# Retention heads two at a time on the full 128 partitions, with weights loaded ahead and filler matmuls in the chunk loop

## The chip, the cores and the metric

One Trainium2 chip, eight cores, each running the same program on its own prompt and its own 16 samples; the cores do not talk to each other. The metric is device time of the slowest core in microseconds (us). PE is the matmul engine, DVE the vector engine, ACT the scalar engine, POOL and SP the engines that here mostly issue transfers. The chip has two dies of four cores. In some executions the cores of a die run at a lower granted PE clock ("slow state") and the time is some per cent longer (in before's profiled run 6862.7 us at 0.777 on one die, 6735.6 us at 0.800 on the other).

## The reference, cut to what matters

Two layers of a decoder. Each layer is: half-step SwiGLU, token mixer (three head groups: gated delta net, a linear recurrent unit, retention), half-step SwiGLU. Only retention is touched. It has four heads of width 64:

```python
rq = rope(ret_q); rk = rope(ret_k) * 64 ** -0.5; rv = ret_v       # 4 heads x 64
o = exp(G) * (q @ S0) + ((q @ k.T) * decay_mask) @ v              # per chunk, G = cumulated log gamma
S = exp(G_C) * S0 + (k * exp(G_C - G)).T @ v                      # 64 x 64 state per head
o = (o - mean(o)) * rsqrt(var(o) + eps) * silu(ret_g)             # per head
out = concat(o_dn, o_lru, o_ret) @ w_out
```

A core has 2080 columns: 2064 prompt tokens (17 chunks, 16 + 16 x 128) and 16 one-token samples with states of their own.

## The kernel before: the parts that matter

Heads are processed one after another. Each uses 64 of the 128 partitions, so the projections fill 64 of the array's 128 columns, and most chunk matmuls 64 of its 128 rows. A fence (everything waits for the last instruction of every engine and every transfer) ends each head.

```python
for h in range(4):
    ...
    for (which, dst, name) in ((0, rq, "rq"), (1, rk, "rk")):       # q and k, with a swapped copy for the rotation
        sl = cnt["w"] % 2                                           # two weight buffers
        P.dma("pool", wring[:, sl, :, 0:64],   wiv[:, :, c0:c0 + 64], w=[("wr", sl)])
        P.dma("pool", wring[:, sl, :, 64:96],  wiv[:, :, c0 + 32:c0 + 64], r=[("wr", sl)], w=[("wr", sl)])
        P.dma("pool", wring[:, sl, :, 96:128], wiv[:, :, c0:c0 + 32], r=[("wr", sl)], w=[("wr", sl)])
        for ti, (a, n) in enumerate(TT):                            # 5 tiles of 416 columns
            for c in range(8): mm(pb[0:64, 0:n],  wring[:, sl, c, 0:64],   xn[:, c, a:a + n], ...)
            for c in range(8): mm(pb2[0:64, 0:n], wring[:, sl, c, 64:128], xn[:, c, a:a + n], ...)
            ...                                                     # three DVE operations: rotate
    def ret_chunk(ci, g):                                           # generator; three chunks in flight
        tr(bank[0:C, 0:64], rk[0:64, ...]); tr(bank[0:C, 64:128], rv[0:64, ...])
        mm(bank[0:C, 128:128 + C], rk[0:64, ...], rq[0:64, ...])    # scores
        yield
        ...                                                         # DVE: scaled k, v, masked scores
        while rturn["i"] != ci: yield                               # chunks take the state in turn
        mm(bank[0:64, 0:C], Sr, qp, start=True, stop=False)
        mm(bank[0:64, 0:C], vtm, MT, start=False, stop=True)
        mm(bank[0:64, 256:320], ktm, vtm)
        yield
        stt(Sr, Sr, gam ** C, bank[0:64, 256:320], ...)             # DVE: new state
        ...                                                         # norm: two means on PE, DVE, ACT
    run_pool(ret_chunk, 17, 3)
    ...                                                             # sample step, then the gate projection
    P.fence()
apply_wout([768, 832, 896, 960], 64)                                # four products over 64 rows
```

Of the kernel before, what the change touches and what calls it, by code (L numbers as in the profile page):

```python
# [10 lines left out]
AF = mybir.ActivationFunctionType  # L11
# [263 lines left out]
def build(stage=99):  # L275
# [18 lines left out]
    c_retdec = din("c_retdec", [4, 128, 128]); c_reteg = din("c_reteg", [64, 4, 128])  # L294
    c_retkd = din("c_retkd", [128, 8]); c_cos = din("c_cos", [64, NT]); c_sin = din("c_sin", [64, NT])
# [12 lines left out]
    with ExitStack() as st:  # L308
# [17 lines left out]
        def mm(out, lhsT, rhs, r, w, start=True, stop=True):  # L326
            P.op("pe", lambda e: e.matmul(out, lhsT, rhs, start=start, stop=stop), r, w)  # L327

# [158 lines left out]
        def mixer(l, xn):  # L487
# [8 lines left out]
            wiv = win[l].rearrange("(c p) n -> p c n", p=128)  # L496
            cnt = {"w": 0, "pre": 0, "tmp": 0, "st": 0}

            def load_w(col0, ncols):
                sl = cnt["w"] % 2  # L500
                cnt["w"] += 1
                P.dma("pool", wring[:, sl, :, 0:ncols], wiv[:, :, col0:col0 + ncols], w=[("wr", sl)])
                return sl

            def proj_tile(sl, ncols, ti):
                a, n = TT[ti]
                pb, kb = PB()
                for c in range(8):
                    mm(pb[0:ncols, 0:n], wring[:, sl, c, 0:ncols], xn[:, c, a:a + n], [("wr", sl), ("xn", ti)], kb,
                       start=(c == 0), stop=(c == 7))  # L510
                return pb, kb
# [444 lines left out]
            apply_wout([512, 640], 128)  # L956
            A.phase("lru")
# [9 lines left out]
            reteg = A.alloc([4, 128])  # L967
            P.dma("sp", reteg[0:64], c_reteg, w=["reteg"])
            for h in range(4):
                mh = A.mark()  # L970
                gam = 1.0 - 2.0 ** (-5.0 - h)
                mrr = AR.mark()
                rq = AR.alloc([NT]); rk = AR.alloc([NT]); rv = A.alloc([NT])
                decT = A.alloc([128])
                P.dma("sp", decT, c_retdec[h], w=["decT"])
                Sr = A.alloc([64])
                memset(Sr[0:64], 0.0, ["Sr"])
                tq_ = A.alloc([2, 512])
                for (which, dst, name) in ((0, rq, "rq"), (1, rk, "rk")):
                    c0 = 2568 + which * 256 + h * 64  # L980
                    sl = cnt["w"] % 2
                    cnt["w"] += 1
                    P.dma("pool", wring[:, sl, :, 0:64], wiv[:, :, c0:c0 + 64], w=[("wr", sl)])
                    P.dma("pool", wring[:, sl, :, 64:96], wiv[:, :, c0 + 32:c0 + 64], r=[("wr", sl)], w=[("wr", sl)])
                    P.dma("pool", wring[:, sl, :, 96:128], wiv[:, :, c0:c0 + 32], r=[("wr", sl)], w=[("wr", sl)])
                    for ti, (a, n) in enumerate(TT):
                        pb, kb = PB()
                        for c in range(8):
                            mm(pb[0:64, 0:n], wring[:, sl, c, 0:64], xn[:, c, a:a + n], [("wr", sl), ("xn", ti)], kb,
                               start=(c == 0), stop=(c == 7))  # L990
                        pb2, kb2 = PB()
                        for c in range(8):
                            mm(pb2[0:64, 0:n], wring[:, sl, c, 64:128], xn[:, c, a:a + n], [("wr", sl), ("xn", ti)], kb2,
                               start=(c == 0), stop=(c == 7))
                        s2 = ti % 2
                        rs = rcnt["i"] % 2
                        rcnt["i"] += 1
                        P.dma("sp", cosr[0:64, rs, 0:n], c_cos[:, a:a + n], w=[("cosr", rs)])
                        P.dma("sp", sinr[0:64, rs, 0:n], c_sin[:, a:a + n], w=[("sinr", rs)])
                        tt(tq_[0:64, s2, 0:n], pb[0:64, 0:n], cosr[0:64, rs, 0:n], ALU.mult, kb + [("cosr", rs)], [("tq", s2)])  # L1000
                        tt(dst[0:64, a:a + n], pb2[0:64, 0:n], sinr[0:64, rs, 0:n], ALU.mult, kb2 + [("sinr", rs)], ck(name, a, a + n))
                        tt(dst[0:64, a:a + n], dst[0:64, a:a + n], tq_[0:64, s2, 0:n], ALU.add, ck(name, a, a + n) + [("tq", s2)],
                           ck(name, a, a + n))
                sl = load_w(3080 + h * 64, 64)
                for ti, (a, n) in enumerate(TT):
                    pb, kb = proj_tile(sl, 64, ti)
                    cp(rv[0:64, a:a + n], pb[0:64, 0:n], kb, ck("rv", a, a + n), eng="act")

                RNG = 3
                rsets = [{k: A.alloc([128]) for k in ("qp", "ktm", "vtm", "MT", "o", "cen")} for _ in range(RNG)]  # L1010
                for T_ in rsets:
                    T_["sq"] = T_["o"]
                    T_["rn"] = T_["o"]
                RAL = {"sq": "o", "rn": "o"}

                def ret_post(o_src, ko, t0, C, T_, K, bank, kbk):
                    cp(T_["o"][0:64, 0:C], o_src, ko, K("o"))
                    yield
                    mm(bank[0:64, 0:C], o64, T_["o"][0:64, 0:C], K("o") + ["o64"], kbk)
                    yield  # L1020
                    tt(T_["cen"][0:64, 0:C], T_["o"][0:64, 0:C], bank[0:64, 0:C], ALU.subtract, K("o") + kbk, K("cen"))
                    tt(T_["sq"][0:64, 0:C], T_["cen"][0:64, 0:C], T_["cen"][0:64, 0:C], ALU.mult, K("cen"), K("sq"))
                    yield
                    mm(bank[0:64, 0:C], o64, T_["sq"][0:64, 0:C], K("sq") + ["o64"], kbk)
                    yield
                    ts(T_["rn"][0:64, 0:C], bank[0:64, 0:C], EPS, -0.5, ALU.add, ALU.pow, kbk, K("rn"))
                    yield
                    tt(oT[0:64, h, t0:t0 + C], T_["cen"][0:64, 0:C], T_["rn"][0:64, 0:C], ALU.mult, K("cen") + K("rn"),
                       ck(("oT", h), t0, t0 + C))
# [3 lines left out]
                def ret_chunk(ci, g):  # L1033
# [6 lines left out]
                    tt(T_["qp"][0:64, 0:C], rq[0:64, t0:t0 + C], reteg[0:64, h, 0:C], ALU.mult, kq_ + ["reteg"], K("qp"), eng="pool")  # L1040
                    tr(bank[0:C, 0:64], rk[0:64, t0:t0 + C], ident[0:64, 0:64], kk_ + ["ident"], kbk)
                    tr(bank[0:C, 64:128], rv[0:64, t0:t0 + C], ident[0:64, 0:64], kv_ + ["ident"], kbk)
                    mm(bank[0:C, 128:128 + C], rk[0:64, t0:t0 + C], rq[0:64, t0:t0 + C], kk_ + kq_, kbk)
                    yield
                    kcol = retkd[0:C, 2 * h + (0 if C == 128 else 1):2 * h + (0 if C == 128 else 1) + 1]
                    ts(T_["ktm"][0:C, 0:64], bank[0:C, 0:64], kcol, None, ALU.mult, None, kbk + ["retkd"], K("ktm"))
                    cp(T_["vtm"][0:C, 0:64], bank[0:C, 64:128], kbk, K("vtm"))
                    tt(T_["MT"][0:C, 0:C], bank[0:C, 128:128 + C], decT[0:C, 0:C], ALU.mult, kbk + ["decT"], K("MT"))
# [3 lines left out]
                    mm(bank[0:64, 0:C], Sr[0:64, 0:64], T_["qp"][0:64, 0:C], ["Sr"] + K("qp"), kbk, start=True, stop=False)  # L1052
                    mm(bank[0:64, 0:C], T_["vtm"][0:C, 0:64], T_["MT"][0:C, 0:C], K("vtm") + K("MT"), kbk, start=False, stop=True)
                    mm(bank[0:64, 256:320], T_["ktm"][0:C, 0:64], T_["vtm"][0:C, 0:64], K("ktm") + K("vtm"), kbk)
                    yield
                    stt(Sr[0:64, 0:64], Sr[0:64, 0:64], gam ** C, bank[0:64, 256:320], ALU.mult, ALU.add, ["Sr"] + kbk, ["Sr"])
                    rturn["i"] = ci + 1
                    yield from ret_post(bank[0:64, 0:C], kbk, t0, C, T_, K, bank, kbk)

                run_pool(ret_chunk, 17, RNG)  # L1060
                P.dma("sp", o_ret_p[l, h], Sr[0:64, 0:64], r=["Sr"], is_out=True)

# [4 lines left out]
                S0r = cosr.rearrange("p a (b c) -> p (a b) c", c=64)  # L1067
                Snr = sinr.rearrange("p a (b c) -> p (a b) c", c=64)
                KS0 = [("cosr", 0), ("cosr", 1)]
                KSN = [("sinr", 0), ("sinr", 1)]  # L1070
                P.dma("sp", S0r[0:64], sret[l, :, h].rearrange("s d e -> d s e"), w=KS0)
                pqs, kpqs = PQ()
                for s in range(16):
                    mm(pqs[0:64, s:s + 1], S0r[0:64, s, :], rq[0:64, NP + s:NP + s + 1], KS0 + ksq, kpqs)
                tt(T_["sq"][0:64, 0:16], rq[0:64, sc_], rk[0:64, sc_], ALU.mult, ksq + ksk, K("sq"))
                pqk, kpqk = PQ()
                mm(pqk[0:64, 0:16], ones_f[0:64, 0:64], T_["sq"][0:64, 0:16], K("sq") + ["ones_f"], kpqk)
                stt(T_["cen"][0:64, 0:16], pqk[0:64, 0:16], 0.125, rv[0:64, sc_], ALU.mult, ALU.mult, kpqk + ksv, K("cen"))
# [156 lines left out]
```

## Time and profile before

| | us |
|---|---|
| three runs | 6798, 6928, 6965 |
| undisturbed runs seen later, in four batches (7 of them, 6735 to 6740, beside the control run) | 6735 to 6746 |
| retention with its output product, both layers, slowest core | 1236 of 6872 |

The prediction shows the lines of the profiled run, on the slowest core, whose die was in the slow state. The same stretches on core 0, whose die was not, are the ones to hold the result against (columns: from:to, width, busy time and count of PE, weight load, DVE, ACT, POOL, then granted clock, DMA share, GB/s):

```profile
2180.30:2193.50 13.20, 0.09 (x1) 0.12 (x2) 0.11 (x1) 0.00 (x0) 3.53 (x4) 0.56 0.74 74
2193.50:2231.40 37.90, 37.90 (x201) 22.89 (x202) 17.49 (x30) 1.99 (x4) 3.89 (x6) 0.93 0.34 54
2231.40:2289.10 57.70, 53.01 (x233) 36.65 (x232) 28.22 (x130) 11.50 (x32) 7.19 (x15) 0.54 0.04 3
2289.10:2308.20 19.10, 11.87 (x84) 9.31 (x83) 5.72 (x19) 1.92 (x7) 0.00 (x0) 0.50 0.07 15
2308.20:2318.60 10.40, 8.32 (x38) 4.63 (x36) 2.92 (x5) 3.83 (x6) 0.00 (x0) 0.84 0.11 26
```

This is head 0 of layer 0: wait for weights, projections, chunk loop, sample step, gate. They differ from the slow die's by 1.6 us at most (37.9 against 39.5 us for the projections), and the stage as a whole takes 555.4 us here and 557.7 there.

### The profile page before, as it was taken

Reading aid. Unit: us, or ns where it says so; the run is one execution under the profiler, and the core shown is the slowest. Engines: PE = TensorE matmul, PEld = TensorE weight load, DVE = VectorE, ACT = ScalarE, POOL = GpSimd, SP = SyncE. Lnnn points to the kernel's source line nnn. Section 1 sums busy time; section 2 is a strip of 40 time slices with the busy share of each in tenths; the row PEclk is TensorE's granted clock in tenths of the full one; section 3 lists DMA queues with packets and bytes.
Section 4 is the critical chain, followed back from the end, with each engine's and each line's share of the span. In section 5 each row is a group of like instructions: output and inputs, shape, how many; then the busy total and the mean of one; then the engine's idle time right before and its main releaser. Section 6 shows DMA issues by size and latency. Waiting matters only on the chain.

```text
span 6871.7 us, 89814 instructions; the slowest of 8 cores (6722.8 to 6871.7 us)
## 1 busy us (share of the span) xinstructions
PE 5041.1 (73%) x26690; PEld 3158.5 (46%) x26690; DVE 3096.0 (45%) x9064; ACT 1374.2 (20%) x3379; POOL 403.3 (6%) x714
## 2 busy tenths in 40 slices
PE   6996657575744887799799947575666377888993
PEld 3553546363622555355355426354454144544552
DVE  2334647465644343333422356556564443443233
ACT  2112222212122111210211131313221311121112
POOL 0000000000000110000000000000000001100000
PEclk9997879697866666698898868787777666759895
DMA  3220000100011111222222000000001012103211
GB/s 79 35 38 10 7 14 8 20 3 18 9 14 21 21 22 25 31 35 28 34 34 34 13 13 6 15 14 7 14 7 19 4 24 31 30 8 50 34 19 50
DMA packets 280770, 154.47 MB, mean 22 GB/s; under 512 B 137226, under 2 KB 258556, under 8 KB 280268
## 3 DMA queue, kind: packets, MB, share of 16 engines
q0 software_dynamic: 216800, 90.23, 11.4%
q1 hardware_dynamic: 63500, 58.50, 3.0%
q8 instruction: 231, 3.78, 0.2%
q14 instruction: 239, 1.96, 0.1%
HBM read 219.00 MB, written 20.36 MB: 35 GB/s over the span
## 4 chain that ended last, share of the span: by engine, by line
PE 60%; DVE 20%; issue 7%; ACT 6%; DMA 5%; DVEq 1%; SPq 0%; POOL 0%; ACTq 0%; POOLq 0%
PE psb L327 58%; DVE arena L356 9%; DVE arena L336 2%; DMA arena<-win 2%; DVE arena L351 2%; DVE rrarena L336 2%; PE psb L330 2%; DVE rrarena L362 2%; ACT arena L333 1%; ACT arena L341 1%; DVE rrarena L356 1%; ACT arena L342 1%; DVE rrarena L351 1%; DVEq L166 1%; ACT L333 1%
## 5 line engine op out<-in xcount | busy, mean ns | idle before, releaser
L327 PE MATMUL psb<-arena 128*128 128x416 bf16 (+10 forms) x18960 | 3938.8, 366 | 1255.5 <-ACT arena L333 405.5
L327 PEld LDWEIGHTS psb<-arena 128*128 128x128 bf16 (+7 forms) x18960 | 2172.2, 127 | 2988.4 <-issue 1840.0
L327 PE MATMUL psb<-rrarena 128*128 128x128 f32 (+4 forms) x6384 | 993.0, 298 | 160.2 <-DVE rrarena L336 126.2
L327 PEld LDWEIGHTS psb<-rrarena 128*128 128x128 f32 (+4 forms) x6384 | 866.3, 206 | 236.6 <-issue 217.6
L336 DVE TENSOR_TENSOR arena<-arena,psb 128x416 bf16<-128x416 f32 (+2 forms) x584 | 296.8, 508 | 1137.4 <-PE psb L327 1136.3
L356 DVE SCALAR_TENSOR_TENSOR arena<-psb,arena 128x416 f32<-128x416 f32 (+1 forms) x1032 | 567.7, 551 | 468.6 <-PE psb L327 436.1
L356 DVE SCALAR_TENSOR_TENSOR arena<-arena 128x416 f32<-128x416 f32 (+4 forms) x1024 | 542.6, 530 | 264.2 <-ACT arena L342 156.5
L333 ACT ACTIVATE arena<-psb 128x416 f32<-128x416 f32 (+3 forms) x656 | 306.1, 467 | 1673.1 <-PE psb L327 1659.3
L360 ACT COPY arena<-psb 128x416 f32<-128x416 f32 (+8 forms) x475 | 174.8, 376 | 1817.6 <-PE psb L327 1241.7
L362 DVE COPY rrarena<-psb 128x128 f32<-128x128 f32 (+2 forms) x1720 | 426.3, 280 | 240.4 <-PE psb L327 230.7
L330 PE MATMUL psb<-arena 128*128 128x128 f32 (+7 forms) x666 | 181.6, 356 | 349.0 <-DMA arena<-sdnc 115.0
L333 ACT ACTIVATE arena<-arena 128x128 f32<-128x128 f32 (+8 forms) x1027 | 307.0, 356 | 573.1 <-DVE arena L356 348.7
L336 DVE TENSOR_TENSOR arena<-arena 128x416 f32<-128x416 f32 (+10 forms) x574 | 241.0, 425 | 376.2 <-ACT arena L333 253.9
L330 PEld LDWEIGHTS psb<-arena 128*128 128x128 f32 (+7 forms) x666 | 115.7, 187 | 383.0 <-issue 380.1
L341 ACT ACTIVATE arena<-psb,arena 128x128 f32<-128x128 f32 (+3 forms) x415 | 174.7, 421 | 583.8 <-PE psb L327 469.3
L362 DVE COPY arena<-psb 128x64 f32<-128x64 f32 (+7 forms) x549 | 145.9, 266 | 222.1 <-PE psb L330 159.8
L356 DVE SCALAR_TENSOR_TENSOR arena<-arena,psb 128x128 f32<-128x128 f32 (+2 forms) x416 | 129.7, 313 | 238.5 <-PE psb L327 199.8
L336 DVE TENSOR_TENSOR rrarena<-rrarena,psb 128x128 f32<-128x128 f32 (+1 forms) x792 | 209.4, 273 | 7.0 <-PE psb L327 6.2
L333 ACT ACT_TABLE_LOAD x93 | 119.3, 1283 | 455.5 <-PE psb L327 307.3
L105 POOL DMA_DIRECT2D arena<-win x106 | 93.9, 888 | 1623.5 <-DVE arena L365 837.5
L336 DVE TENSOR_TENSOR arena<-psb,arena 128x128 f32<-128x128 f32 (+5 forms) x276 | 93.2, 338 | 212.7 <-PE psb L327 206.0
L351 DVE TENSOR_SCALAR rrarena<-psb,arena 128x128 f32<-128x128 f32 (+1 forms) x408 | 130.2, 346 | 103.3 <-PE psb L327 73.7
(39 smaller groups left out, 1457.3 us busy)
## 6 DMA issues: line engine op xcount, KB each, us to landing
arena<-w1i POOLq DMA_DIRECT2D x44, 512.0 KB, 9.7
arena<-w2i POOLq DMA_DIRECT2D x44, 512.0 KB, 8.1
arena<-w1o POOLq DMA_DIRECT2D x44, 256.0 KB, 8.3
arena<-w2o POOLq DMA_DIRECT2D x44, 256.0 KB, 7.7
arena<-win POOLq DMA_DIRECT2D x40, 256.0 KB, 4.6
arena<-c_cos SPq DMA_DIRECT2D x80, 104.0 KB, 2.5
arena<-c_sin SPq DMA_DIRECT2D x80, 104.0 KB, 2.8
arena<-xp SPq DMA_DIRECT2D x16, 512.0 KB, 4.0
```

The costliest lines, as they stand in the source:

```text
L105: return e.dma_start(out=out, in_=in_, **kw)
L166: eng.wait_ge(s, v)
L327: P.op("pe", lambda e: e.matmul(out, lhsT, rhs, start=start, stop=stop), r, w)
L330: P.op("pe", lambda e: e.transpose(out, in_, idn), r, w)
L333: P.op("act", lambda e: e.activation(out, in_, func, bias=bias, scale=scale), r, w)
L336: P.op(eng, lambda e: e.tensor_tensor(out, a, b, op), r, w)
L341: P.op("act", lambda e: e.activation(out, a, AF.Ln, bias=epsc[0:out.shape[0], :], scale=1.0), list(r) + ["epsc"], w)
L342: P.op("act", lambda e: e.activation(out, out, AF.Exp, scale=-0.5), w, w)
L351: P.op(eng, lambda e: e.tensor_scalar(out, a, s1, None, op0), r, w)
L356: P.op(eng, lambda e: e.scalar_tensor_tensor(out, a, s, b, op0, op1), r, w)
L360: P.op("act", lambda e: e.copy(out, in_), r, w)
L362: P.op(eng, lambda e: e.tensor_copy(out, in_), r, w)
```

## The change

The intent: process heads in pairs, so that four passes become two and partitions, array rows and array columns are full; load the weights of a pair ahead of it; and issue throw-away matmuls in the chunk loop, which are meant to keep PE's clock up. The diff, cut to its core (`[...]` marks cuts; mechanical changes from `[0:64, ...]` to `[:, ...]` are left out):

```diff
+        def warm(k, n=512):
+            for _ in range(k):
+                mm(psb[7][:, 0:n], xn[:, 0, 0:128], xn[:, 1, 0:n], [("xn", 0), ("xn", 1)], [("psb", 7)])
[...]
+            slots += [oT[:, i, k * 1024:(k + 1) * 1024].rearrange("p (c n) -> p c n", c=8) for i in (2, 3) for k in range(2)]
+            def pair_loads(hp):        # 12 loads: q, q swapped (4 pieces), k, k swapped (4), v, gate
[...]
+            for x in pair_loads(0):    # issued before the fence that starts retention
+                ld(*x)
[...]
-            for h in range(4):
+            for hp in range(2):
[...]
-                    tr(bank[0:C, 0:64], rk[0:64, t0:t0 + C], ident[0:64, 0:64], kk_ + ["ident"], kbk)
[...]
+                    if hp == 0 and 3 <= ci < 14:
+                        ld(*pair_loads(1)[ci - 3])
+                    tr(bank[0:C, 0:128], rk[:, t0:t0 + C], ident, kk_ + ["ident"], kbk)
+                    tr(bank[0:C, 128:256], rv[:, t0:t0 + C], ident, kv_ + ["ident"], kbk)
+                    scb = [(bank[0:C, 256:256 + C], kbk), (psb[g][0:C, 0:C], [("psb", g)])]
+                    for hh in range(2):
+                        b0 = hh * 64
+                        mm(scb[hh][0], rk[b0:b0 + 64, t0:t0 + C], rq[b0:b0 + 64, t0:t0 + C], kk_ + kq_, scb[hh][1])
+                    warm(2)
[...]
+                    mm(bank[:, 0:C], Sr, T_["qp"][:, 0:C], ...)           # block-diagonal 128 x 128 state
+                    for hh in range(2): mm(bank[b0:b0 + 64, 0:C], T_["vtm"][0:C, b0:b0 + 64], T_["MT%d" % hh], ...)
+                    for hh in range(2): mm(bank[b0:b0 + 64, 256 + b0:320 + b0], T_["ktm"][...], T_["vtm"][...], ...)
+                    warm(1)
[...]
+                if hp == 0:
+                    ld(*pair_loads(1)[11])                                 # gate weights of pair 1
[...]
-            apply_wout([768, 832, 896, 960], 64)
+            apply_wout([768, 896], 128)
```

## The prediction

> **What bounds the kernel now.** I read the list of cores first, then the page, then the DMA issues by their source tensor to find where the changed stage (the retention heads) lies, then a table of stretches over one head, and last the groups by form inside the stage.
>
> ```profile
> die 0 (median of its cores): 6735.6 us, clock 0.800
> die 1 (median of its cores): 6862.7 us, clock 0.777
> ```
>
> The profiled run is a slow one. The times of before are 6798, 6928 and 6965 us, so the median of 6928 us is probably slow too (my reading: 1.9% above the fastest).
>
> The rotary tables and the retention states are loaded only by this stage. Their first and last issues put retention, on the slowest core, at 2190 to 2748 us in layer 0 and 5541 to 6094 us in layer 1. Its output product follows until 2809.6 and 6157.8 us. Together that is 619.3 + 616.6 = 1236 us, 18% of the span. Nothing else runs beside it, for a fence stands before and after. So the change is worth what this stage gets shorter. Head 0 of layer 0 splits into these stretches (columns: width, busy time of PE, weight load, DVE, ACT, POOL, then granted clock, DMA share, GB/s):
>
> ```profile
> 2190.30:2203.40 13.10, 0.00 (x0) 0.03 (x1) 0.11 (x1) 0.00 (x0) 3.53 (x4) 0.53 0.75 75
> 2203.40:2242.90 39.50, 39.49 (x205) 23.55 (x206) 17.50 (x30) 2.27 (x5) 3.89 (x6) 0.90 0.33 52
> 2242.90:2301.00 58.10, 53.34 (x228) 36.89 (x228) 28.31 (x130) 11.21 (x32) 7.20 (x15) 0.53 0.04 3
> 2301.00:2320.20 19.20, 11.78 (x82) 9.31 (x82) 5.63 (x19) 1.92 (x7) 0.00 (x0) 0.50 0.07 15
> 2320.20:2331.10 10.90, 8.82 (x38) 4.83 (x36) 2.92 (x5) 3.83 (x6) 0.00 (x0) 0.80 0.10 25
> 2748.00:2809.60 61.60, 55.99 (x160) 23.38 (x160) 23.65 (x40) 0.00 (x0) 2.10 (x4) 0.53 0.05 9
> 2155.00:2190.30 35.30, 24.39 (x80) 6.31 (x80) 23.54 (x40) 0.00 (x0) 0.00 (x0) 0.73 0.08 15
> 1080.00:1205.00 125.00, 92.77 (x689) 82.22 (x688) 91.48 (x397) 26.07 (x104) 11.31 (x26) 0.99 0.00 1
> ```
>
> In order: a bare wait for weights, the q/k/v projections, the chunk loop, the sample step, the gate projection, and retention's output product; the last two are other stages, for comparison: the recurrent unit's output product, and the delta net's chunk loop. The reader is to see two things. In the chunk loop PE is busy for 53.3 of 58.1 us at a clock of 0.53, so it is bound by a PE at half speed. And the product over 64 rows takes 160 matmuls in 56 us, also at 0.53, while the one over 128 rows takes 80 in 24 us and reaches more. The groups by form show the widths:
>
> ```profile
> L327 PE MATMUL psb<-arena 128*64 128x416 bf16 x960 | 189.7, 364 | 64.7 <-DMA arena<-win 64.7
> L327 PE MATMUL psb<-arena 64*64 64x128 f32 x384 | 117.0, 426 | 19.7 <-DVE arena L336 11.2 <-DVE arena L362 4.4 <-DVE arena L356 1.7
> L327 PE MATMUL psb<-arena 64*128 64x416 bf16 x160 | 56.0, 550 | 6.8 <-DMA arena<-wout 6.7
> ```
>
> 960 projection matmuls fill only 64 of 128 columns, the chunk matmuls 64 rows, and PE stands 64.7 us per layer for projection weights.
>
> [...]activity over 64 rows does not count as enough: the 64-row product ran 56 us without a gap at 0.53, and the chunk loop fell to 0.50 although PE was busy. [...]the recurrent unit's product stands at 0.81 from 2165 us on[...]. [...]The 64 KB weight pieces (128 B rows at the source) land in 3.3 us and the 256 KB ones (512 B rows) in 4.6 us at the median[...].
>
> **The change, part by part, per layer.** Two heads share the 128 partitions, so four passes become two. Before, the four heads took 557.7 us in layer 0.
>
> *Projections.* Before 4 x 39.3 = 157 us. After, a pair needs 5 tiles x (16 + 16 + 8) = 200 matmuls of 128x128 by 416, as many as a head had. [...]I take 0.205 us: 41 us a pair, 82 us. DVE has 30 operations of 0.58 us, 17.5 us, hidden. Saved 75 us.
>
> *Chunk loop.* Before 4 x 57.2 = 229 us. After, per chunk, PE work at full clock: one f32 matmul of 128 columns goes as two records of about 0.107 us (before: 0.213 us each at half clock). Two transposes 0.43, two score products 0.43, state x q 0.21, two v x mask 0.43, two k x v 0.21, two means 0.43, three warm matmuls of 512 columns 0.64: 2.78 us. The old sum is 1.39 us at full or 2.77 us at half clock, and the loop took 57.2/17 = 3.36 us, so 82% of the time was nominal PE work. DVE rises from 8 to 11 operations a chunk; at the delta net's pace (397 operations in 125 us, 0.315 us each) that is 3.5 us. In that loop PE's 689 records x 0.107 make 59% of the time. If the clock holds, 59% to 82% gives 3.4 to 4.7 us and DVE says 3.5 us; I choose 3.9 us, 66 us a pair, 132 us a layer. Saved 97 us.
>
> *Will the clock hold?* [...]I think it holds, with chance 0.85. The warm matmuls touch a bank that nothing else uses in the loop, so they cost PE time only.
>
> *Sample step.* Before 4 x 19.1 = 76 us. After, the state load is issued ahead of the loop (2.2 us of wait gone), the 16 small products become 32 (3.5 us more, as PE is bound by weight loads there), the masked keys are twice as wide (1.3 us), the outer products twice as many (3.5 us): 25 us, 50 us a layer. Saved 26 us.
>
> *Gate.* Before 4 x 10.6 = 42 us, after 2 x 11.5 = 23 us, cold start included. Saved 19 us.
>
> *Weight waits.* Before, the rest of 557.7 us: 53 us. After, pair 0's 12 loads are issued at about 2155 us, beside the recurrent unit's product, which lasts 35 us. [...]Eleven of pair 1's loads go out in the loop and are hidden. The gate's own slot is reloaded only after the last gate matmul, and a fence makes everyone wait for it: 4.6 us less about 1.5 us of tail. With start-up 6 us in all. Saved 47 us.
>
> *Output product.* Before 61.6 us; after, 80 matmuls over 128 rows, as in the recurrent unit, where it took 39 us with its load wait and DVE set the pace at 0.76 us a group. Saved 22 us.
>
> Sum: 75 + 97 + 26 + 19 + 47 + 22 = 286 us a layer; both layers are alike within 5 us, so 570 us. From 6928 us that gives 6358 us, from the fast 6798 us 6228 us.
>
> **The rivals.** First: the clock drops in the chunk loop in spite of the warm matmuls. For it: [...]the loop is full of short waits. Then the nominal 5.56 us at 82% is 6.8 us a chunk, 115 us a pair, no gain in the loop and 196 us back: about 6550 us. Second: DVE becomes the bound. For it: its work per chunk grows by 3/8, and it was busy for 28 of 58 us at half the PE pace. At 4.6 us a chunk I lose 12 us a pair, 48 us in all: about 6405 us. Third: pair 0's loads outlast the product beside them, since 8 of 12 have 128 B rows and the fence waits for all. At the software queue's mean of 58 ns a packet (11.4% of 16 x 6872 us over 216800 packets) 12 x 1024 packets take 44.5 us, 9 us too long: 20 us in all. Fourth, upwards: products on disjoint halves of the array overlap, and a chunk takes 3.3 us: 40 us better.
>
> **Range and chances.** The slow and fast states lie 130 us apart, and the loop is worth 50 us either way; I put the middle at 6340 us, a little under the slow figure, and 6190 to 6460 us around it. Even the cold loop saves over 2%, so faster has 0.97, same 0.02, slower 0.01.
>
> **What would show it.** In the changed profile: retention near 290 us a layer and its product near 40; the loop's clock at 0.9 or more and 3.9 us between chunks; projections at 0.81 to 1.0 and 0.17 to 0.21 us a matmul; PE's wait for projection weights down from 64.7 to about 6 us a layer. A loop at 0.5, or a wait of over 10 us ahead of pair 0, would prove me wrong.

## The result

| | before | after |
|---|---|---|
| median of 14 runs, us | 6913.59 | 6150.63 |
| lowest to highest | 6741.35 to 7056.47 | 6110.89 to 6532.73 |
| ratio of fast runs | | 0.9017 (95%: 0.8966 to 0.9067) |

A ratio is the mean time of one kernel's fast runs over that of the other's of the same rounds, so it is not quite the ratio of the medians. The ratio still holds some state: five of the 14 runs of before count as fast and spread over 1.3%, while seven of after's eight fast runs lie between 6111 and 6116 us (the eighth, at 6185, is the profiled one). In the later batches before also ran undisturbed, at 6735 to 6746 us, and a repeat of after ran at 6105 to 6113 us. In the batch of that repeat the means of the undisturbed runs are 6737.5 and 6108.7 us, so the gain is about 629 us, a ratio of 0.907. On core 0 of the two profiled runs, each on a die that was not in the slow state, the spans are 6732.0 and 6107.6 us: 624 us.

The cores of the changed kernel's profiled run:

```profile
die 0 (median of its cores): 6099.3 us, clock 0.835
die 1 (median of its cores): 6158.8 us, clock 0.821
```

Core 0, layer 0, in the changed kernel: the recurrent unit's output product with pair 0's loads beside it, projections, chunk loop, sample step, gate, and the wait before pair 1:

```profile
2145.90:2179.10 33.20, 21.83 (x80) 6.37 (x80) 23.56 (x40) 0.00 (x0) 6.69 (x8) 0.91 0.83 51
2179.10:2217.80 38.70, 36.81 (x201) 19.93 (x202) 17.90 (x34) 2.02 (x4) 1.04 (x3) 0.96 0.52 130
2217.80:2276.00 58.20, 49.99 (x386) 33.55 (x384) 43.19 (x180) 11.25 (x32) 16.66 (x25) 1.00 0.42 24
2276.00:2295.50 19.50, 11.80 (x144) 10.42 (x143) 7.01 (x20) 1.90 (x7) 0.00 (x0) 0.65 0.02 4
2295.50:2306.00 10.50, 8.84 (x41) 4.31 (x40) 3.71 (x6) 3.76 (x6) 0.94 (x1) 0.84 0.23 51
2306.00:2311.20 5.20, 0.00 (x0) 0.00 (x0) 0.00 (x0) 0.00 (x0) 0.00 (x0) 0.80 0.58 50
```

Read line by line against head 0 above: each stretch takes about as long as it did for one head, and now serves two. The 13 us wait in front is gone, and 5 us of it stand at the end of pair 0. The loop has a clock of 1.00 in place of 0.54.

The whole stage, both layers, then retention's output product with the norm that follows (up to the next FFN's first weight load); before first, core 0:

```profile
2180.30:2735.70 555.40, 443.64 (x2200) 294.35 (x2200) 217.98 (x736) 76.74 (x196) 58.20 (x101) 0.67 0.20 27
5433.80:5988.50 554.70, 443.31 (x2200) 293.88 (x2200) 218.10 (x735) 76.94 (x196) 57.73 (x100) 0.67 0.20 27
2735.70:2842.70 107.00, 73.88 (x200) 26.74 (x200) 49.72 (x80) 24.76 (x51) 2.08 (x4) 0.51 0.04 5
```

and after:

```profile
2179.10:2439.60 260.50, 217.89 (x1534) 138.68 (x1534) 142.95 (x475) 38.07 (x98) 26.34 (x46) 0.90 0.29 50
5117.50:5385.90 268.40, 226.93 (x1534) 145.38 (x1534) 143.18 (x475) 38.17 (x98) 26.39 (x46) 0.86 0.27 48
2439.60:2520.30 80.70, 39.31 (x120) 10.20 (x120) 49.64 (x80) 24.76 (x51) 1.16 (x2) 0.71 0.04 7
```

The stage saves 294.9 and 286.3 us, and the output product 26.3 in layer 0 and 25.1 in layer 1 (106.0 to 80.8, read the same way): 633 us together. The span of core 0 shrinks by 624, so all of the gain is here, and the rest of the kernel is some 9 us longer in sum.

The groups by form answer to the three that the prediction shows. The two kinds with 64 columns or 64 rows that were costliest are gone; this is layer 0 on the slowest core (partitions x elements, count, busy us and mean ns, idle time before and what ended it):

```profile
L328 PE MATMUL psb<-arena 128*128 128x416 bf16 x564 | 116.4, 362 | 27.8 <-DVE arena L370 9.6 <-DVE arena L361 7.5 <-issue 6.9
L328 PE MATMUL psb<-arena 128*128 128x128 f32 x192 | 41.8, 308 | 17.7 <-DVE arena L367 6.7 <-DVE arena L341 5.5 <-DVE arena L361 5.4
L328 PE MATMUL psb<-arena 128*128 128x512 bf16 x102 | 34.9, 397 | 0.0
```

The first row counts projections and output product together; no transfer is named any more among the leading causes of its idle time. That is in part only the name: the waits put down to DVE L370 and to "issue" stand behind fences, and the last runs below shorten both by loading weights earlier. The third are the warm matmuls, 51 a pair.

### The profile page after: what moved, and what is told of

The parts are those of the page before. It is cut to its first block, busy times and chain, and to the rows that moved or that the text cites.

```text
span 6183.6 us, 84250 instructions; the slowest of 8 cores (6096.6 to 6183.6 us)
## 1 busy us (share of the span) xinstructions
PE 4479.2 (72%) x25198; PEld 2813.4 (45%) x25198; DVE 2949.0 (48%) x8542; ACT 1296.5 (21%) x3183; POOL 359.1 (6%) x626
## 4 chain that ended last, share of the span: by engine, by line
PE 59%; DVE 22%; issue 8%; ACT 6%; DMA 4%; DVEq 1%; SPq 0%; ACTq 0%; POOL 0%; POOLq 0%
PE psb L328 57%; DVE arena L361 11%; DVE arena L341 2%; DVE rrarena L341 2%; DVE arena L356 2%; DVE rrarena L367 2%; PE psb L335 2%; ACT arena L338 1%; ACT arena L346 1%; DVE rrarena L361 1%; ACT arena L347 1%; DVEq L166 1%; DVE rrarena L356 1%; DMA arena<-win 1%; ACT L338 1%
## 5 line engine op out<-in xcount | busy, mean ns | idle before, releaser
L328 PE MATMUL psb<-arena 128*128 128x416 bf16 (+8 forms) x17356 | 3426.8, 353 | 1134.9 <-ACT arena L338 407.7
L328 PEld LDWEIGHTS psb<-arena 128*128 128x128 bf16 (+4 forms) x17356 | 1862.4, 120 | 2652.8 <-issue 1577.0
L341 DVE TENSOR_TENSOR arena<-arena,psb 128x416 bf16<-128x416 f32 (+1 forms) x512 | 278.1, 543 | 1074.9 <-PE psb L328 1073.1
L338 ACT ACTIVATE arena<-psb 128x416 f32<-128x416 f32 (+2 forms) x636 | 295.8, 466 | 1604.9 <-PE psb L328 1597.8
L365 ACT COPY arena<-psb 128x416 f32<-128x416 f32 (+6 forms) x451 | 164.8, 374 | 1572.8 <-PE psb L328 1143.4
L335 PE MATMUL psb<-arena 128*128 128x128 f32 (+5 forms) x594 | 159.2, 362 | 342.9 <-DMA arena<-sdnc 110.3
L341 DVE TENSOR_TENSOR arena<-arena 128x416 f32<-128x416 f32 (+8 forms) x394 | 182.1, 466 | 300.3 <-ACT arena L338 226.8
L335 PEld LDWEIGHTS psb<-arena 128*128 128x128 f32 (+5 forms) x594 | 97.0, 178 | 380.4 <-issue 373.6
L346 ACT ACTIVATE arena<-psb,arena 128x128 f32<-128x128 f32 (+2 forms) x343 | 150.0, 437 | 389.3 <-PE psb L328 254.9
L367 DVE COPY arena<-psb 128x128 f32<-128x128 f32 (+5 forms) x413 | 119.1, 289 | 218.2 <-PE psb L335 154.6
```

The source lines that it names most:

```text
L328: P.op("pe", lambda e: e.matmul(out, lhsT, rhs, start=start, stop=stop), r, w)
L335: P.op("pe", lambda e: e.transpose(out, in_, idn), r, w)
L338: P.op("act", lambda e: e.activation(out, in_, func, bias=bias, scale=scale), r, w)
L341: P.op(eng, lambda e: e.tensor_tensor(out, a, b, op), r, w)
L346: P.op("act", lambda e: e.activation(out, a, AF.Ln, bias=epsc[0:out.shape[0], :], scale=1.0), list(r) + ["epsc"], w)
L365: P.op("act", lambda e: e.copy(out, in_), r, w)
```

## The experiments

The theory to test was the prediction's: the loop is faster because PE runs at full clock, the warm matmuls hold that clock, and what counts for the clock is full-height work. The rivals: pairing alone holds the clock; the clock alone, without pairing, gives the gain; prefetching gives it. "Undisturbed" below means the fast runs that cluster within 0.3%; the changed kernel's are 6105 to 6116 us, and the differences below are taken from their middle, 6111. The batches ran on four chips, but before ran undisturbed at 6735 to 6742 us on three of them and at 6742 to 6746 on that of the six-warm run. Loop lines are from core 0, one or more of its four loops, in the columns above. The changed kernel's four loops:

```profile
2217.80:2276.03 58.23, 50.02 (x386) 33.55 (x384) 43.22 (x180) 11.25 (x32) 16.66 (x25) 1.00 0.42 24
2348.82:2408.25 59.43, 51.44 (x386) 34.39 (x384) 43.16 (x180) 11.30 (x32) 6.66 (x14) 0.97 0.01 1
5155.62:5217.15 61.53, 53.81 (x386) 36.27 (x384) 43.40 (x180) 11.36 (x32) 16.71 (x25) 0.92 0.38 23
5291.88:5353.44 61.56, 54.05 (x386) 36.41 (x384) 43.28 (x180) 11.24 (x32) 6.66 (x14) 0.92 0.01 1
```

Even here the clock slips now and then, and a loop at 0.92 takes 3.3 us more than one at 1.00.

### Without the warm matmuls

```diff
-                    warm(2)
-                    warm(1)
```

> The changed kernel without its three warm matmuls per chunk. Theory A (the warm matmuls hold the clock): the loop falls to a granted clock of 0.5; nominal PE work 2.14 us at full, 4.28 us at half clock, at 82% gives 5.2 us a chunk, 89 us a pair instead of 58, so 4 x 31 = about 120 us longer than the changed kernel (near 6235 us in the fast state). Theory B (the full-height f32 matmuls that pairing brought hold it alone): clock stays at 1.0, the loop shrinks to 50 to 55 us a pair, 15 to 30 us shorter in all.

Measured: 6170 to 6179 us in the three undisturbed runs, 62 us more than the changed kernel's 6111.

```profile
2213.03:2285.05 72.02, 66.01 (x335) 47.12 (x333) 43.75 (x180) 11.68 (x32) 16.45 (x25) 0.54 0.32 19
2362.52:2434.76 72.24, 66.80 (x335) 47.83 (x333) 43.80 (x180) 11.68 (x32) 6.46 (x14) 0.52 0.00 1
```

The clock drops to 0.52 to 0.54 and stays there: theory A in kind, theory B is out. The size is half of what A said, because the cold loop takes 72 us and not 89. So pairing is worth most of the loop's gain by itself: four loops of 58 us become two of 72, which saves 87 us a layer, and the clock another 24 (two of 60).

### Warm matmuls over 64 rows

```diff
-                mm(psb[7][:, 0:n], xn[:, 0, 0:128], xn[:, 1, 0:n], ...)
+                mm(psb[7][:, 0:n], xn[0:64, 0, 0:128], xn[0:64, 1, 0:n], ...)
```

> The warm matmuls kept in number and length, but over 64 rows of the array instead of 128 (same PE time). Theory A (activity is weighed by the rows in use): the clock is lost or flickers in the loop; if all lost, 5.56 us of nominal work at 82% is 6.8 us a chunk, 115 us a pair, about 230 us longer than the changed kernel. Theory B (time busy counts, whatever the rows): clock 1.0 and 58 us a pair, time as the changed kernel.

Measured: 6212 to 6219 us undisturbed, 104 us more.

```profile
2218.90:2306.26 87.36, 85.38 (x385) 50.83 (x383) 43.93 (x180) 11.57 (x32) 16.64 (x25) 0.53 0.27 16
2381.25:2468.24 86.99, 84.69 (x385) 50.33 (x383) 43.97 (x180) 11.57 (x32) 6.63 (x14) 0.54 0.00 1
5215.24:5287.40 72.16, 67.84 (x386) 41.19 (x384) 43.39 (x180) 11.56 (x32) 16.61 (x25) 0.74 0.32 19
```

PE is busy 98% of the loop, more than in any other chunk loop shown here, and its clock is 0.53. So it is not the time that PE is busy that holds the clock; three of four loops were cold, one was cold for part (0.74). A half-height filler is worse than none, at 87 us a cold loop against 72: it costs its time and earns nothing. (With it the loop also changes more often between matmuls of 64 and of 128 rows; this run does not separate the two. The output product over 64 rows below keeps one form, 64*128, all the way and is cold too, at 0.50, so such changes are not needed for that.)

### One warm matmul, and six

```diff
-                    warm(2)          # one_warm: only the later one stays
```

```diff
-                    warm(2)          # six_warm: 4 and 2 in place of 2 and 1
+                    warm(4)
-                    warm(1)
+                    warm(2)
```

> The changed kernel with one warm matmul per chunk (the one after the state products) instead of three. Without any the loop ran at 0.53 and 72 us, with three at 0.92 to 1.00 and 58 to 62 us. Theory A (a threshold of full-height activity lies between): the clock flickers, 0.6 to 0.9, and the loop takes 62 to 70 us, 15 to 40 us longer in all than the changed kernel. Theory B (one is enough): clock 0.95 or more, and the loop 55 to 58 us, up to 20 us shorter in all.

> The changed kernel with six warm matmuls per chunk (four and two) instead of three. Theory A (PE's own time sets the loop's pace even at full clock, so every warm matmul is paid): 3 x 0.213 us x 17 chunks, about 11 us a pair longer, 69 to 72 us a loop, about 40 us longer in all. Theory B (a fifth of PE's time in the loop is slack, the pace comes from the chain between PE, DVE and ACT): under 4 us a pair, with the clock at 1.00 throughout.

One: 6128 to 6137 us, 21 us more. Six: 6133 to 6150 us, 29 us more, of which some 6 may be the chip, as before was longer by that there. A loop of each, one warm first:

```profile
2212.82:2273.58 60.76, 48.48 (x346) 35.44 (x350) 43.06 (x180) 11.21 (x32) 16.45 (x25) 0.86 0.39 23
```

```profile
2216.89:2282.19 65.30, 59.84 (x437) 38.73 (x435) 43.61 (x180) 11.24 (x32) 16.58 (x25) 1.00 0.36 21
```

With one, the clock flickers (0.83 to 0.86 over the four loops), theory A; the loops take 60.7 to 61.8 us, a bit better than A said. With six it is 1.00 in all four loops, and they take 65.0 to 65.8 us: 7 us over a three-warm loop at 1.00. The 51 added matmuls are 11.0 to 11.5 us of PE time, at the 0.215 to 0.226 us that one takes from start to start in the changed kernel's loop at 1.00, so about two thirds are paid and one third falls into PE's gaps. That lies between the two theories: PE's order is most of what sets the pace, but not all. Of the four numbers tried (0, 1, 3 and 6) three is the best.

### Warm matmuls in the one-head kernel

The kernel before with `warm(2)` after its score product and `warm(1)` after its state products.

> The kernel before, one head at a time, with the same three warm matmuls per chunk and nothing else changed. Theory A (the clock alone is worth much of the loop's gain): clock near 1.0, a chunk needs 2.03 us nominal, 42 to 50 us a head instead of 57, 60 to 120 us shorter than before in all. Theory B (pairing is needed, since the one-head loop has too little full-height work): the clock stays at 0.5, nominal 4.05 us at 82% is 4.9 us a chunk, 84 us a head, about 215 us longer than before.

Measured: 6879 to 6884 us undisturbed, against 6738: 144 us longer.

```profile
2238.20:2304.11 65.91, 62.87 (x282) 33.94 (x281) 28.36 (x130) 11.28 (x32) 7.35 (x15) 0.71 0.04 3
2385.45:2461.71 76.26, 74.21 (x282) 39.70 (x281) 28.46 (x130) 11.49 (x32) 7.34 (x15) 0.57 0.03 3
```

Theory B: the clock is lost in five of the eight loops (0.57) and comes and goes in the other three (0.71). The same filler that helps the paired loop harms the one-head loop, where the state and the means are 64 rows high. Even where the clock came up to 0.71 the loop took 66 us instead of 58. So the filler needs the pairing; the pairing does not need the filler, as the run without it showed.

### No prefetch

```diff
+                for x in pair_loads(hp):     # at the start of each pair; all other load sites removed
+                    ld(*x)
```

> The changed kernel with all twelve weight loads of a pair issued at the start of that pair, none ahead. Theory A (issuing them without waiting for one another already takes out most of the old wait): PE waits about 8 us at the start of each pair, 22 us longer in all (0.4%). Theory B (only the prefetch hides them): the old 13 us a pair come back, or more as the swapped pieces are four loads, about 40 us longer or above.

Measured: 6136 to 6144 us undisturbed, 30 us more, between the two theories. PE starts pair 0 with waits of 7.8 and 1.7 us for weights and pair 1 with 7.1 and 7.8. So the prefetch is worth about 0.5%, and less than the 47 us a layer that the prediction booked under waits: the rest probably went because loads are no longer chained to one another and come twice, not four times, per layer, which was not tested apart.

### The output product over 64 rows

```diff
-                        for i in range(npc):
-                            mm(pb[:, 0:n], womix[0:kparts, i, ...], oT[0:kparts, i, a:a + n], ...)
+                        prs = [(i, p0) for i in range(npc) for p0 in ((0, 0) if split else (0,))]   # lower half twice: wrong on purpose
+                        for j_, (i, p0) in enumerate(prs):
+                            p1 = p0 + 64 if split else kparts
+                            mm(pb[:, 0:n], womix[p0:p1, i, ...], oT[p0:p1, i, a:a + n], ...)
```

> The changed kernel with retention's output product over 64 rows again, as 160 matmuls instead of 80 (the lower half twice: a wrong result on purpose[...]). Theory A (the product gained its 22 us a layer by matching the array's height, in count and in clock): it takes 60 us a layer again at a clock near 0.53, and the whole is about 45 us longer. Theory B (half the gain was the clock it inherits from a busier stage): clock 0.8 or above[...], about 30 to 35 us, no loss.

The result is wrong, as intended. Measured: 6158 and 6173 us in the two fast runs, about 54 us more. The matmuls of the product on PE (start, width, form, count), and the granted clock of a stretch inside:

```profile
2449.24 55.62 PE L328 MATMUL psb<-arena 64*128 64x416 bf16 x160 [7.43 <-DMA arena<-wout]
```

```profile
2450.00:2500.00 50.00, 50.00 (x146) 20.62 (x145) 21.23 (x36) 0.00 (x0) 0.00 (x0) 0.50 0.00 1
```

against the changed kernel's

```profile
2445.20:2480.00 34.80, 23.64 (x86) 6.60 (x86) 23.59 (x40) 2.96 (x7) 0.00 (x0) 0.89 0.00 1
```

Theory A. PE is busy without a gap and still at half clock, 0.50, for 50 us. With 128 rows the clock is 0.89 on average, and DVE sets the pace: two matmuls start every 0.76 us, after a wait for DVE of 0.25 us.

### One DVE operation moved to ACT

```diff
-                    cp(T_["vtm"][0:C, :], bank[0:C, 128:256], kbk, K("vtm"))
+                    cp(T_["vtm"][0:C, :], bank[0:C, 128:256], kbk, K("vtm"), eng="act")
```

> One of the eleven DVE operations of a chunk (the copy of the transposed values, 0.28 us) goes to ACT, which is busy 11 of 58 us there. Theory A (DVE, at 43 of 58 us, shares in setting the loop's pace, as the prediction's second rival had it): the loop drops by 1 to 4 us a pair, 5 to 15 us in all. Theory B (PE order and the chain between engines set it): no change, within 1 us a pair, or a little longer[...].

Measured: one fast run only, 6136 us. The four loops took 62.0, 62.9, 65.4 and 62.3 us with the clock at 0.92 to 1.00; at 1.00 that is 3.8 us longer than the changed kernel's 58.2.

```profile
2217.51:2279.50 61.99, 49.14 (x378) 33.38 (x384) 40.57 (x163) 15.75 (x49) 16.64 (x25) 1.00 0.39 22
```

DVE lost 2.7 us of work and the loop got longer, by 3.8 us where theory B allowed 1 us or a little more. The trace shows that the move did more than lighten DVE: in this loop the moved copies waited 9.1 us for DVE's scaling of the keys, and DVE's masking waited 7.8 us for the copies, a wait that the changed kernel does not have. So the run put ACT into DVE's chain, and it does not show whether less DVE work alone would help; DVE's load, 74% of the loop, stays open as a part of what bounds it.

### The waits that are left

```diff
+            slots.append(AR.t[...])                       # slot6: a buffer of its own for pair 1's gate weights
-                if hp == 0: ld(*pair_loads(1)[11])        # now in the loop with the other eleven
```

and, in best_a, also the two weight blocks of retention's output product, loaded in pair 1's loop; best_b adds 28 warm matmuls in each sample step.

> A sixth buffer for pair 1's gate weights, loaded in the loop like the others, so that no load stands in front of the fence between the pairs. If that load is all that the 5.2 us gap between the pairs is, the gap falls below 1 us and the whole by about 10 us (6103 us in the fast state). Rival: the rotary tables that pair 1 needs first land only 6 us after the fence anyway, PE runs out of banks, and half or more of it comes back.

> The changed kernel with pair 1's gate weights in a buffer of their own and with the output product's two weight blocks also loaded in pair 1's loop. Theory: the two waits that are left in front of fences go, 5 us between the pairs and about 5 us before the output product, so 20 us in all: about 6093 us. Rival: the waits were beside other tails (the silu and product chain of the gate), and under 10 us come out.

> The same with 28 more warm matmuls in each sample step, put where PE waits for DVE (6, 12 and 10). Theory A (they hold the clock over the sample step, which runs at 0.65 on average): the outer products go from 3.3 to about 2 us and the gate starts at full clock, 3 to 5 us a pair, 12 to 20 us better than the run before this in the list. Theory B (too little full-height work, or they come in the way of the chain in PE's order): clock still 0.5 to 0.7 and 1 to 3 us a pair longer.

> The changed kernel as it is, as a control on the chip of the next two: about 6113 us in its fast runs, loops of 58 to 62 us with the clock between 0.92 and 1.00, changing from run to run.

PE's first matmuls of pair 1 in the changed kernel, then in slot6 (idle time before them in brackets):

```profile
2311.48 13.77 PE L328 MATMUL psb<-arena 128*128 128x416 bf16 x65 [7.14 <-DVE arena L370]
```

```profile
2306.74 5.79 PE L328 MATMUL psb<-arena 128*128 128x416 bf16 x32 [2.62 <-DVE arena L370]
```

slot6 ran at 6103 and 6106 us undisturbed, some 7 us better than 6111, which by itself is hardly outside the changed kernel's own spread; the evidence is the trace. There the gap falls by 4.5 us and not to nothing, as the gate's tail on ACT and DVE is left. And 1.46 us come back after these 32 matmuls, in a wait for DVE, which had itself waited 6.82 us for a rotary table. Over half of the gap is left, as the rival said. best_a ran at 6093 and 6095 us beside a control (after_again) at 6105 to 6113: 15 us better, against 20 expected. PE's idle time before the output product falls from 7.47 to 2.62 us. But the intervals of the ratios (0.8995 to 0.9127 for best_a, 0.9005 to 0.9097 for the control) do not separate the two: a third run of best_a, 6156 us with one die longer, also counts as fast. That it is faster rests on two undisturbed runs and on the gaps in the trace. It is correct and, by these two runs, the fastest correct kernel here, by 0.2%.

best_b gave a wrong result: as the code reads, the filler writes a bank in which the sample step can hold sums that are still to be read. Its timing can still be read with that reservation: 6095 to 6103 us in the undisturbed runs, no better than best_a. The sample step of pair 0 took 24.1 us at a clock of 0.72, against 22.0 at 0.56, and the gate 8.5 us against 10.8. What the gate won, the filler had cost: theory B by sum.

## Why the prediction was right or wrong

The direction, the place and the order of the parts were right, and the relative gain (0.9017 of 6928 is 6247 us) lies in the range. As an absolute time the median, 6150.63 us, lies 39 us below the range's lower end. Two things made that up, and both are sizes; one step of the mechanism failed besides, the price of a cold loop (below).

*The state.* The prediction took 6798 us for before's fast time and thought the median of the changed kernel would be a slow one. Undisturbed before is 6738 us, and after ran fast in eight of 14 runs. With 6738 in place of 6798 its own 570 us would have given 6168 us. That the relative figure lies in the range is no merit of the sum either: 570 us fell short of the 624 measured, and the range was wide enough.

*The savings, per layer.* Measured on core 0, mean of the two layers:

| part | before, as predicted from | after, predicted | after, measured |
|---|---|---|---|
| projections | 157 | 82 | 76.0 |
| chunk loop | 229 | 132 | 120.4 |
| sample step | 76 | 50 | 41.8 |
| gate | 42 | 23 | 21.3 |
| waits | 53 | 6 | 5.1 |
| output product, saved | | 22 | 25.8 |

- *Chunk loop, 11.6 us too much.* The term that was off is the "3.9 us" a chunk: 120.4/34 = 3.54 us was measured. Part of it is the PE sum of 2.78 us. In the trace of a chunk, two transposes start 0.11 and 0.20 us apart (0.31 us together, not 0.43), so the sum is 2.66; and PE's nominal share is 2.66/3.42 = 78% in a loop at clock 1.00, where the prediction, with 3.9 us out of a stretch of 59% to 82%, had taken 71%. "DVE says 3.5" was no bound: at clock 1.00 a chunk took 3.42 us, so the second rival (4.6 us) did not come. The score products show nothing won by the fourth rival's overlap either: on the two halves of the rows they take 0.43 us (third and fourth line below), as booked.

```profile
2259.56 0.27 PE L335 MATMUL psb<-arena,rrarena 128*128 128x128 f32 x1
2259.67 0.27 PE L335 MATMUL psb<-arena 128*128 128x128 f32 x1
2259.87 0.49 PE L328 MATMUL psb<-rrarena 64*128 64x128 f32 x4
2260.30 0.61 PE L328 MATMUL psb<-arena 128*128 128x512 bf16 x2
```

- *"Will the clock hold?"* Right, and shown: with three warm matmuls 0.92 to 1.00, with one 0.83 to 0.86, with none 0.52 to 0.54. That three would do was the estimate: by the prediction's own times 1.92 us (0.21 + 0.43 + 0.21 + 0.43 + 0.64) of a chunk's 3.9 us are full-height work, 49%, and no trace of before shows what share is needed. The runs with fewer show that the kernel is near an edge. What failed is the first rival's price of a cold loop, and with it the idea that the loop's whole gain hangs on the clock. A loop with the warm matmuls at half clock is what the half-height filler gives: 87 us a pair, where the rival said 115 and "no gain in the loop"; two of 87 are still less than four of 58. Without filler a cold loop takes 72 us, so pairing alone brings 87 of the 111 us a layer. The rival took a cold PE at 82% of nominal; the loop without filler ran at 95% (2.02 us nominal at full, 4.04 at half, 4.24 measured, with the transposes at 0.31). PE was busy 92% of it, so little of the chain between the engines shows.
- *Projections, 6 us too much.* "0.205 us" a matmul, the estimate, was wrong: 168 of them took 29.70 us, 0.177 us each, at a clock of 1.00. On this die the four pairs took 36.6 to 38.0 us at 0.94 to 0.96. On core 5, on the other die of the same run, three of the four pairs did so too (37 to 38 us at 0.92 to 0.96); the fourth took 42.4 us at 0.82, about the 41 us predicted.
- *Sample step, 8 us too much.* The prediction added "3.5 us more" for twice as many small products at the old pace. But the loop's end now leaves PE at a higher clock: 64 records took 2.03 us at 1.00 in pair 0 of layer 0, and 3.0 to 3.5 us in the other three pairs, where 32 had taken 3.5 at 0.50 (beside weight loads that were busy for 3.49 us). So the clock won here as well, which the prediction had not seen.
- *Waits:* right to the us, and the cause as said in the main: 5.2 us at the end of pair 0, and a buffer of its own took 4.5 us off PE's gap there. The third rival (loads that outlast the product beside them) did not come: on core 0 pair 0's twelve loads were issued from 2142.0 to 2153.1 us, the DMA share was 0.00 from 2165 us on, and the product beside them ran until 2176 us, so the projections started with no wait for a transfer. No experiment says which part of the old 53 us each cause held; without prefetch about 30 us of both layers return.
- *Output product:* right, and 4 us better than said.
- *Row length of the loads:* an effect of it is not shown. Pieces of 64, 128 and 256 KB landed in 3.3, 3.8 and 4.6 us in before; row length and size grow together here, so nothing tells them apart.

What stays open: what exactly sets the loop's pace at full clock. It is not PE's time alone (two thirds of added PE time are paid), and DVE's load was not tested cleanly. In 45 us of a loop at 1.00 PE's waits are put down to DVE's element-wise products and differences (1.9 us), its copies (1.8) and its state update (1.6), so no one DVE operation stands out; the chain of state product, DVE update and next state product was not tried by itself.

## What to carry to other kernels

When a loop is bound by PE at half clock, ask how high its matmuls are before asking how busy PE is: packing two heads onto 128 rows both halves the work and makes filler count (a clock of 0.92 to 1.00, against 0.52 to 0.54 without filler), and filler without the packing made things worse (144 us longer). Price the filler by removing it, cutting it and doubling it: here too few let the clock flicker (0.83 to 0.86 with one) and too many were paid for at two thirds (7 of 11.0 to 11.5 us a loop). And read absolute times by state: here two of three known runs were slow, and that cost the prediction about as much (60 us) as all its mis-sized terms together (63 us).

## What the traces show of PE's clock

- Height counts. 160 matmuls over 64 rows ran 55.6 us without a gap at a clock of 0.50, and a loop with PE busy 98% of the time stayed at 0.53 with 64-row filler, while 64 columns with 128 rows ran at 0.93 on average (head 0's projections).
- The clock of the same dense matmuls differed between the dies: in before's profiled run core 0 ran 400 us of FFN matmuls at 1.00, and the other three cores of its die stood at 1.00 too from 2925 to 3300 us, while core 4, on the other die, ran its FFN at 0.92 and stood at 0.81 in the recurrent unit's product. In slices of 20 us that 0.92 is 1.00 up to 3065 us, 0.81 from 3085 to 3225, and 1.00 again from 3245. All eight cores ran the same program. So in this run the slow state shows as stretches at 0.81 that come and go on one die, while the other stood at 1.00; no run here tests what sets it off:

```profile
2900.00:3300.00 400.00, 400.00 (x2277) 222.58 (x2276) 135.04 (x230) 48.10 (x93) 22.64 (x32) 1.00 0.23 32
```

```profile
2925.00:3325.00 400.00, 400.00 (x2116) 216.03 (x2115) 122.10 (x207) 44.98 (x87) 20.89 (x30) 0.92 0.23 32
```

- What share of full-height work holds the clock in a loop with gaps is known here only at the points tried. By the prediction's times at full clock (1.28 us a chunk for the f32 products, 0.21 us a filler; the transposes are left out), three fillers a chunk are 1.92 of 3.42 us (56% of 58.2/17 us) and hold it at 0.92 to 1.00; one filler is 1.49 of 3.58 us (42% of 60.8/17 us) and gives 0.83 to 0.86. The recurrent unit's product, two matmuls of 0.176 us every 0.76 us, is at about 46% and ran at 1.00 (core 0 of the changed kernel, 2153 to 2176 us). All three shares are estimates.
